# Differential-attention scores as K=64 products on two halves of the array, and the value products ordered by operand

## Chip, cores and metric

The kernel runs on one core of a Trainium2 chip. The metric is the device time of one execution in microseconds.

## What is computed

One inference step of a two-layer encoder for 1024 prompt frames and 32 sample frames, with `D_MODEL` = 1024. Layer 0 mixes tokens by causal pooling, layer 1 by differential attention; both layers also attend to 256 memory tokens, and both end in a squared-ReLU MLP. The change lies in layer 1's differential attention on the prompt:

```python
def diff_core(q, k, v, q_pos, k_pos, lam, slopes):
    """q (B,Tq,H,2,d), k (B,Tk,H,2,d), v (B,Tk,H,2d). Returns (A1 - lam*A2) V, (B,Tq,H,2d)."""
    s = jnp.einsum('bqhcd,bkhcd->cbhqk', q, k).astype(jnp.float32) * (DIFF_HEAD_DIM ** -0.5)
    dist = jnp.abs(q_pos[:, None] - k_pos[None, :]).astype(jnp.float32)
    bias = -slopes[:, None, None] * dist[None]
    vis = (k_pos[None, :] // CHUNK) <= (q_pos[:, None] // CHUNK)
    s = jnp.where(vis, s + bias, -jnp.inf)
    p = jax.nn.softmax(s, axis=-1)
    a = p[0] - lam * p[1]
    return jnp.einsum('bhqk,bkhe->bqhe', a.astype(v.dtype), v)
```

There are 4 heads. Each has two components c = 0, 1 of d = 64 dimensions, so a head's query or key has 128 dimensions, [component 0 | component 1]. A score is a sum over 64 dimensions only; the values have 128.

## The kernel before

**Precision.** TensorE works on a type (`F32R`) that keeps only part of a float32. Every operand is therefore split in a high part, a copy made by ScalarE (ACT), and a low part, the operand less the high one, made by VectorE (DVE) or GpSimd (POOL): `split`, L55. A product is then three matmuls: high x high, high x low, low x high (`mm3`, L48 to L53). The low x low product is left out where `mm3` is used.

**Stages.** `run` (L1586) calls layer 0's mixing (`mix0`), its output projection and MLP (`tail`), then layer 1's mixing (`mix1`, L938) and its `tail`. The change is in `mix1` alone.

**Inside `mix1`.** The work is written as generators, which yield the time that they estimate to have put on TensorE (PE). `drive` (L527) steps through the units, which are the attention (`diff_unit`, L915, then the memory attention), and after each step takes about 0.8 times that estimate from a filler, `fill1` (L959): dense projections of 352 token columns (`g_dense`, L143), in PSUM tiles named `dn`. So scores and values are interleaved with dense work, in one order per engine that is fixed when the program is built; a scheduler still moves instructions past each other in that order.

For each head, `diff_project` (L685) makes keys `kst`, values `vst` and queries. For the queries, one 1024-column tile is kept for 256 tokens: `Q` has the shape [128, 2, 2, 256], for component, part (high, low) and token. Component c is split where it falls, on partitions 64c to 64c+63 (L728), and then copied by a DMA on the SP queue to the other 64 partitions (L734), so that all 128 partitions hold the 64 dimensions twice. `diff_keys` (L739) puts, for each component, the high part of the keys on one half of the partitions and the low part on the other (`KS`, [128, 2, 1024]).

`diff_scores` (L782) goes through blocks i = 0 to 7 of 128 queries, two to a `pair`; block i sees Wi = max(256, 128(i + 1)) keys. For each component it multiplies the stacked parts, so two matmuls of 128 rows give four products, low x low among them:

```python
nc.tensor.matmul(o, lhsT=q[:, c, 0, qc], rhs=KS[:, c, k:k + n], start=True, stop=False)
nc.tensor.matmul(o, lhsT=q[:, c, 1, qc], rhs=KS[:, c, k:k + n], start=False, stop=True)
```

(L799, L800.) Up to 512 keys are one chunk; more are two chunks of Wi/2. Each component takes one PSUM tile `sc` of two banks; there are two such tiles. DVE then adds the distance table and takes the extremum in one instruction (L806), ACT takes the exponential (L808), and `combine` (L777) subtracts the second component's probabilities, scaled, from the first's. A yield stands after each component.

`diff_values` (L823) transposes two blocks' probabilities on PE (L841), splits them into `ah` and `al` (DVE makes `al`), and multiplies with the split values `V` through `mm3`, one key block of 128 after the other: V high x ah, V high x al, V low x ah, then the same for the next block. These matmuls have 256 columns.

**Gates.** With `until`, the filler stops until a named score block is done, since query tiles (`q`, four buffers) must come free. Head h's queries wait pair by pair for head h-1's scores (L718). The memory queries wait at L962.

**Other work in PE's halves.** The sample group's scores (`diff_sample`, L878 and L879) multiply 64 rows at a time, component 0 on the lower half of the array's rows and component 1 on the upper, with 32 columns of weights; L903 uses 32 rows. Everything else of the kernel uses all 128 rows.

Of the kernel before, what the change touches and what calls it, by code (L numbers as in the profile page):

```python
# [9 lines left out]
F32 = mybir.dt.float32  # L10
F32R = mybir.dt.float32r
AF = mybir.ActivationFunctionType
ALU = mybir.AluOpType
# [3 lines left out]
SEQ = 1024  # L17
NS = 32
NT = SEQ + NS
GW = 352  # L20
# [7 lines left out]
SC_DIFF = 64.0 ** -0.5  # L28
# [5 lines left out]
STEPS = 44  # L34
LAG = 22
KEYS_AT = 1
T2_AT, T_AT = 8, 20
ORDER = (2, 0, 1)
YOFF = 896
# [3 lines left out]
class Kern:  # L43
# [292 lines left out]
    def mem_project(self, l, h, p, out, qs, gate=()):  # L336
        nc = self.nc
        W = self.weight()
        for key in gate:
            yield from self.until(key)  # L340
        q = [self.qp.tile([128, 2, 512], F32R, tag="q", name="mq", bufs=self.nq) for a in range(2)]
        for g in range(NG):
            ps = self.dntile()[:, :GW]
            yield from self.g_dense(ps, W, g)
            qf = p.tile([128, GW], F32, tag="qf", name="qf", bufs=2)
            nc.vector.tensor_tensor(qf, ps, self.rs[g], ALU.mult)
            for a, lo, hi in ((0, 0, 512), (1, 512, SEQ)):
                lo, hi = max(lo, g * GW), min(hi, (g + 1) * GW)
                if lo < hi:
                    s = slice(lo - 512 * a, hi - 512 * a)  # L350
                    self.split(q[a][:, 0, s], q[a][:, 1, s], qf[:, lo - g * GW:hi - g * GW], nc.gpsimd)
            if g == NG - 1:
                nc.gpsimd.tensor_copy(qs[:, h, :], qf[:, GW - NS:])
        out[h] = q

    def mem_load_kv(self, l, h, p):
        nc, t = self.nc, self.t
# [327 lines left out]
    def diff_project(self, h, p, out, smp):  # L685
        nc, t = self.nc, self.t
        W = self.weight()
        if h:
            yield from self.until(("ks", h - 1))
        kst = self.pd.tile([128, NT], F32, tag="kst", name="kst", bufs=1)  # L690
        for g in ORDER if h == 0 else range(NG):
            ps = self.dntile()[:, :GW]
            yield from self.g_dense(ps, W, g)
            nc.vector.tensor_tensor(kst[:, g * GW:(g + 1) * GW], ps, self.rs[g], ALU.mult)
        nc.sync.dma_start(t["kT"][h], kst)
        self.kst = kst
        self.done.add(("k", h))

        W = self.weight()
        if h:  # L700
            yield from self.until(("v", h - 1))
        vst = self.pd.tile([128, NT], F32, tag="vst", name="vst", bufs=1)
        for g in range(NG):
            ps = self.dntile()[:, :GW]
            yield from self.g_dense(ps, W, g)
            nc.vector.tensor_tensor(vst[:, g * GW:(g + 1) * GW], ps, self.rs[g], ALU.mult)
        nc.sync.dma_start(t["vT"][h], vst)

        W = self.weight()
        Q = []  # L710
        for g in range(NG):
            ps = self.dntile()[:, :GW]
            yield from self.g_dense(ps, W, g)
            qf = p.tile([128, GW], F32, tag="qf", name="qf", bufs=2)
            nc.vector.tensor_tensor(qf, ps, self.rs[g], ALU.mult)
            lo, end = g * GW, min((g + 1) * GW, SEQ)
            if h:
                yield from self.until(("s", h - 1, (end - 1) // 256))  # L718
            while lo < end:
                n = lo // 256  # L720
                hi = min(end, 256 * (n + 1))
                s = slice(lo - 256 * n, hi - 256 * n)
                if len(Q) == n:
                    Q.append(self.qp.tile([128, 2, 2, 256], F32R, tag="q", name="Q", bufs=self.nq))
                q = Q[n]
                for c in range(2):
                    b = slice(64 * c, 64 * c + 64)
                    self.split(q[b, c, 0, s], q[b, c, 1, s], qf[b, lo - g * GW:hi - g * GW], nc.gpsimd)  # L728
                lo = hi
                if hi == 256 * (n + 1):  # L730
                    qd = q.bitcast(F32)
                    for c in range(2):
                        b, o = slice(64 * c, 64 * c + 64), slice(64 - 64 * c, 128 - 64 * c)
                        nc.sync.dma_start(qd[o, c], qd[b, c])  # L734
            if g == NG - 1:
                nc.gpsimd.tensor_copy(smp["q"][:, h, :], qf[:, GW - NS:])
        out[h] = {"vst": vst, "Q": Q}

    def diff_keys(self, h, smp):  # L739

        nc = self.nc
        while ("k", h) not in self.done:
            yield 0.0
        kst = self.kst
        KS = self.pd.tile([128, 2, SEQ], F32R, tag="ks", name="KS", bufs=2)
        KSf = KS.bitcast(F32)
        for a in range(4):
            s = slice(256 * a, 256 * a + 256)
            nc.scalar.copy(KS[0:64, 0, s], kst[0:64, s])
            nc.scalar.copy(KS[64:128, 1, s], kst[64:128, s])  # L750
            nc.vector.tensor_tensor(KS[64:128, 0, s], kst[0:64, s], KSf[0:64, 0, s], ALU.subtract)
            nc.vector.tensor_tensor(KS[0:64, 1, s], kst[64:128, s], KSf[64:128, 1, s], ALU.subtract)
            yield 0.0
        self.KS[h] = KS
        nc.gpsimd.tensor_copy(smp["k"][:, h, :], kst[:, SEQ:])
        self.done.add(("ks", h))
# [25 lines left out]
    def diff_scores(self, h, pair, p, d, A):  # L782
        nc = self.nc
        Wk = 256 * (pair + 1)
        q = d["Q"][pair]
        KS = self.KS[h]
        for i in (2 * pair, 2 * pair + 1):
            qc = slice((i % 2) * 128, (i % 2) * 128 + 128)
            Wi = max(256, 128 * (i + 1))
            st = self.pd.tile([128, 8], F32, tag="std", name="std", bufs=4)  # L790
            prs = []
            for c in range(2):
                tile = self.sctile()
                n = Wi if Wi <= 512 else Wi // 2
                off = 512 - n if Wi > 512 else 0
                sc = tile[:, off:off + Wi]
                for k in range(0, Wi, n):
                    o = sc[:, k:k + n]
                    nc.tensor.matmul(o, lhsT=q[:, c, 0, qc], rhs=KS[:, c, k:k + n], start=True, stop=False)  # L799
                    nc.tensor.matmul(o, lhsT=q[:, c, 1, qc], rhs=KS[:, c, k:k + n], start=False, stop=True)  # L800
                if c:
                    pr = p.tile([128, Wk], F32, tag="p1", name="pr", bufs=1)
                else:
                    pr = (p if pair % 2 else self.pd).tile([128, Wk], F32, tag=f"pA{2 + pair % 2}", name="pr", bufs=2)
                y = YOFF - 128 * i
                nc.vector.tensor_tensor_reduce(out=pr[:, :Wi], in0=sc, in1=self.dtab[:, y:y + Wi], scale=-SC_DIFF,  # L806
                                               scalar=3e38, op0=ALU.add, op1=ALU.min, accum_out=st[:, c:c + 1])
                self.last_exp = nc.scalar.activation(pr[:, :Wi], pr[:, :Wi], AF.Exp, bias=st[:, c:c + 1],  # L808
                                                     scale=-1.0, accum_out=st[:, 4 + c:5 + c])
                prs.append(pr)  # L810
                if c == 0:
                    yield 0.22 * (pair + 1)
            nc.vector.reciprocal(st[:, 6:8], st[:, 4:6])
            nc.vector.tensor_scalar(st[:, 7:8], st[:, 7:8], self.lam, None, ALU.mult)
            self.combine(p, 128, Wi, prs[0], prs[1], st[:, 6:7], st[:, 7:8])
            if Wi < Wk:
                nc.gpsimd.memset(prs[0][:, Wi:], 0.0)
            A.append(prs[0])
            if i % 2:
                self.done.add(("s", h, pair))  # L820
            yield 0.22 * (pair + 1)

    def diff_values(self, h, pair, p, d, A):  # L823
        nc = self.nc
        V = d["V"]
        nk = 2 * (pair + 1)
        po = None
        for kk in range(0, nk + 2, 2):
            if kk:
                if po is None:  # L830
                    po = self.mmtile()[:, :256]
                for a in range(2):
                    k = kk - 2 + a
                    self.mm3(po, V[:, 0, k, :], V[:, 1, k, :], ah[:, 256 * a:256 * a + 256],
                             al[:, 256 * a:256 * a + 256], k == 0, k == nk - 1)
            if kk < nk:
                pt = self.mmtile()
                for a in range(2):
# [120 lines left out]
    def fill1(self, p, dd, qq, smp, qs):  # L959
        for h in range(4):  # L960
            yield from self.diff_project(h, p, dd, smp)
        gates = [[("s", 3, 1)], [("s", 3, 3)], [("m", 1, 0, 1)], [("m", 1, 1, 1)]]  # L962
        for h in range(4):
            yield from self.mem_project(1, h, p, qq, qs, gates[h])
        self.new_x(1)
# [715 lines left out]
```

## Time and profile before

| what | value |
|---|---|
| median of 3 runs | 2105.55 us (2105.54 to 2108.3) |
| the profiled execution | 2107.0 us |
| its span, first to last instruction | 2105.2 us |
| granted TensorE clock, mean | 0.997 |
| PE busy | 99% of the span, 13068 matmuls |
| DVE, ACT, POOL busy | 80%, 53%, 27% |

How to read it: L12 is line 12 of the kernel. PE is TensorE's matmuls, PEld its weight loads, which can run while an earlier matmul streams. Matmuls are pipelined, and one row's duration runs on while the next has started, so a busy PE is no measure of density: the distance of two starts is. A form like `64*32` behind a matmul says how many rows and columns of the array its weights take; `128x512` is the size of its result. "x12" merges twelve equal instructions, with the time from the first's start to the last's end. Idle time is given with the engine, tile and line that ended it ("<- DVE aTl L57"). `sc`, `mm` and `dn` are the PSUM tiles of scores, of transposes and values, and of dense work.

### The profile page before, as it was taken

The page shows a single profiled execution, that of the slowest core. Times are in us where ns is not written, and L with a number is a line of the kernel's source. Part 1 is how long each engine was busy: PE and PEld are TensorE (multiplying, and loading weights), DVE is VectorE, ACT ScalarE, POOL GpSimd, SP SyncE. Part 2 cuts the span into 40 slices and gives each one's busy share as a digit, 9 for nine tenths or more (in the row PEclk, how much of TensorE's full clock was granted, in tenths as well). Part 3 has the DMA queues.
Part 4 walks back from the last instruction along what each step waited for, and adds up shares of the span by engine and source line. Part 5 has one row for each costly group of instructions (what it writes and reads, how often), then busy time and mean ns, then how long its engine had stood idle before and what let it go on. Part 6 is the DMA issues. An engine that isn't in the chain of part 4 may idle for free. (4 is left out here: it accounts for less than half of the span.)

```text
span 2105.2 us, 35352 instructions
## 1 busy us (share of the span) xinstructions
PE 2081.7 (99%) x13068; PEld 2045.3 (97%) x13068; DVE 1683.4 (80%) x3164; ACT 1125.7 (53%) x2437; POOL 568.0 (27%) x577
## 2 busy tenths in 40 slices
PE   9999999999999999999999999999999999999998
PEld 8998999999999999999999998999999999999997
DVE  8856598888888888868778877589888888888865
ACT  7546365444444444456777766355544444444454
POOL 1021113333333333220111212104334333333323
PEclk9999999999999999999999999999999999999999
DMA  5634411111111111124222213411111111111112
GB/s 192 198 113 139 149 55 56 51 49 53 49 53 45 57 41 60 41 71 159 77 79 79 83 37 99 160 51 51 56 46 54 48 51 51 48 53 50 52 41 83
DMA packets 88269, 156.85 MB, mean 75 GB/s; under 512 B 12832, under 2 KB 30880, under 8 KB 87584
## 3 DMA queue, kind: packets, MB, share of 16 engines
q1 hardware_dynamic: 86224, 149.61, 22.3%
q10 hardware_dynamic: 1872, 4.98, 0.8%
q8 instruction: 102, 1.67, 0.3%
q14 instruction: 71, 0.58, 0.1%
HBM read 126.64 MB, written 23.72 MB: 71 GB/s over the span
## 5 line engine op out<-in xcount | busy, mean ns | idle before, releaser
L51 PE MATMUL dn<-xh,whi 128*128 128x352 f32 x1168 | 383.8, 329 | 2.9 <-ACT xh L229 1.1
L52 PE MATMUL dn<-xl,whi 128*128 128x352 f32 x1168 | 379.0, 324 | 0.4 <-DVE xl L230 0.4
L53 PE MATMUL dn<-xh,wlo 128*128 128x352 f32 x1168 | 378.9, 324 | 0.0
L109 DVE TENSOR_TENSOR wlo<-wraw,whi 128x512 fp32r<-128x512 f32 x344 | 280.1, 817 | 83.6 <-ACT whi L108 82.8
L1375 DVE TENSOR_TENSOR x<-x,mm 128x352 f32<-128x352 f32 x560 | 287.5, 513 | 62.7 <-PE mm L53 62.6
L108 ACT CAST whi<-wraw 128x512 fp32r<-128x512 f32 x344 | 212.4, 620 | 232.4 <-PE dn L52 117.5
L51 PE MATMUL mm<-h2h,whi 128*128 128x352 f32 x832 | 270.4, 325 | 0.0
L53 PE MATMUL mm<-h2h,wlo 128*128 128x352 f32 x832 | 268.0, 322 | 0.0
L52 PE MATMUL mm<-h2l,whi 128*128 128x352 f32 x832 | 266.4, 320 | 0.0
L108 ACT CAST whi<-ws 128x512 fp32r<-128x512 f32 x232 | 143.9, 620 | 220.3 <-PE dn L52 123.4
L1375 DVE TENSOR_TENSOR x<-x,xb 128x352 f32<-128x352 f32 x448 | 222.8, 511 | 26.1 <-PE xb L53 23.4
L51 PEld LDWEIGHTS dn<-xh,whi 128*128 128x128 f32 x1168 | 219.8, 188 | 8.4 <-issue 2.0
L52 PEld LDWEIGHTS dn<-xl,whi 128*128 128x128 f32 x1168 | 221.0, 189 | 3.1 <-DVE xl L230 1.3
L53 PEld LDWEIGHTS dn<-xh,wlo 128*128 128x128 f32 x1168 | 220.4, 189 | 0.4
L57 POOL TENSOR_TENSOR h2l<-t,h2h 128x352 fp32r<-128x352 f32 x112 | 137.0, 1224 | 170.8 <-ACT h2h L56 170.8
L109 DVE TENSOR_TENSOR wlo<-ws,whi 128x512 fp32r<-128x512 f32 x232 | 179.0, 772 | 3.5 <-ACT whi L108 3.5
L57 POOL TENSOR_TENSOR h2l<-b,h2h 128x352 fp32r<-128x352 f32 x92 | 116.2, 1275 | 228.7 <-PE mm L53 204.0
L1359 POOL TENSOR_TENSOR t<-b,b 128x352 f32<-128x352 f32 x56 | 64.7, 1155 | 366.3 <-ACT b L1278 366.3
L52 PEld LDWEIGHTS mm<-h2l,whi 128*128 128x128 f32 x832 | 156.3, 188 | 0.4
L51 PEld LDWEIGHTS mm<-h2h,whi 128*128 128x128 f32 x832 | 156.1, 188 | 0.4
L53 PEld LDWEIGHTS mm<-h2h,wlo 128*128 128x128 f32 x832 | 156.2, 188 | 0.0
L53 PE MATMUL dn<-T,wlo 128*128 128x352 f32 x480 | 155.7, 324 | 0.0
(312 smaller groups left out, 5326.9 us busy)
## 6 DMA issues: line engine op xcount, KB each, us to landing
wraw<-in_w_ff SPq DMA_DIRECT2D x256, 256.0 KB, 2.6
wraw<-in_w_out SPq DMA_DIRECT2D x44, 256.0 KB, 3.6
wraw<-in_w_mem SPq DMA_DIRECT2D x32, 256.0 KB, 3.1
wraw<-in_w_in SPq DMA_DIRECT2D x30, 256.0 KB, 3.1
o<-oscr SPq DMA_DIRECT2D x36, 176.0 KB, 3.0
xscr<-x SPq DMA_DIRECT2D x3, 1408.0 KB, 4.7
wraw<-in_w_kv SPq DMA_DIRECT2D x16, 256.0 KB, 2.6
Q<-Q SPq DMA_DIRECT2D x32, 128.0 KB, 2.2
```

The source lines that it names most:

```text
L51: mm(ps, lhsT=ah, rhs=bh, start=first, stop=False, skip_group_check=more)
L52: mm(ps, lhsT=ah, rhs=bl, start=False, stop=False, skip_group_check=more)
L53: self.last_mm = mm(ps, lhsT=al, rhs=bh, start=False, stop=last, skip_group_check=more)
L57: (lo_eng or self.nc.vector).tensor_tensor(lo, src, hi.bitcast(F32), ALU.subtract)
L108: self.nc.scalar.copy(hi, src)
L109: eng.tensor_tensor(lo, src, hi.bitcast(F32), ALU.subtract)
L1359: self.nc.gpsimd.tensor_tensor(h[out], h[a], h[c], ALU.subtract)
L1375: nc.vector.tensor_tensor(xj, xj, ps, ALU.add)
```

## The change

Queries and keys are no longer stacked. `Q` is [128, 2, 512], high and low for 512 tokens, split over all 128 partitions at once (the helper `split_q`, cut out of `mem_project`); the copies between halves are gone. `KS` is split the same way, in two pieces of 512 keys. A score now takes three products of 64 rows for each component, high x high, high x low, low x high; the two components stand on rows 0 to 63 and 64 to 127, and are issued in turn, each into its own PSUM bank. Low x low is no longer part of it. Both components are issued before the first of them is read; up to 512 keys they share one `sc` tile, above that they take both. The yields change from 0.22 to 0.25 per pair index. The gates follow the two query tiles a head: head h's queries wait for head h-2's last pair, and the first memory queries for head 2's last pair. `diff_values` writes its products by operand: V high x ah for both key blocks, V low x ah for both, V high x al for both.

```diff
+Y0, Y1 = 0.25, 0.25
...
+    def split_q(self, q, qf, g):
+
+        for a, lo, hi in ((0, 0, 512), (1, 512, SEQ)):
+            lo, hi = max(lo, g * GW), min(hi, (g + 1) * GW)
+            if lo < hi:
+                s = slice(lo - 512 * a, hi - 512 * a)
+                self.split(q[a][:, 0, s], q[a][:, 1, s], qf[:, lo - g * GW:hi - g * GW], self.nc.gpsimd)
...
-        Q = []
+        if h > 1:
+            yield from self.until(("s", h - 2, 3))
+        Q = [self.qp.tile([128, 2, 512], F32R, tag="q", name="Q", bufs=self.nq) for a in range(2)]
...
-                for c in range(2):
-                    b = slice(64 * c, 64 * c + 64)
-                    self.split(q[b, c, 0, s], q[b, c, 1, s], qf[b, lo - g * GW:hi - g * GW], nc.gpsimd)
-                lo = hi
-                if hi == 256 * (n + 1):
-                    qd = q.bitcast(F32)
-                    for c in range(2):
-                        b, o = slice(64 * c, 64 * c + 64), slice(64 - 64 * c, 128 - 64 * c)
-                        nc.sync.dma_start(qd[o, c], qd[b, c])
+            self.split_q(Q, qf, g)
...
-        for a in range(4):
-            s = slice(256 * a, 256 * a + 256)
-            nc.scalar.copy(KS[0:64, 0, s], kst[0:64, s])
-            nc.scalar.copy(KS[64:128, 1, s], kst[64:128, s])
-            nc.vector.tensor_tensor(KS[64:128, 0, s], kst[0:64, s], KSf[0:64, 0, s], ALU.subtract)
-            nc.vector.tensor_tensor(KS[0:64, 1, s], kst[64:128, s], KSf[64:128, 1, s], ALU.subtract)
+        for a in range(0, SEQ, 512):
+            s = slice(a, a + 512)
+            self.split(KS[:, 0, s], KS[:, 1, s], kst[:, s])
...
+            if Wi > 512:
+                sc = [self.sctile()[:, 512 - n:512 - n + Wi] for c in range(2)]
+            else:
+                tile = self.sctile()
+                sc = [tile[:, 512 * c:512 * c + Wi] for c in range(2)]
+            for k in range(0, Wi, n):
+                for m, (u, v) in enumerate(((0, 0), (0, 1), (1, 0))):
+                    for c in range(2):
+                        b = slice(64 * c, 64 * c + 64)
+                        nc.tensor.matmul(sc[c][:, k:k + n], lhsT=q[b, u, qc], rhs=KS[b, v, k:k + n],
+                                         start=m == 0, stop=m == 2)
...
-                for k in range(0, Wi, n):
-                    o = sc[:, k:k + n]
-                    nc.tensor.matmul(o, lhsT=q[:, c, 0, qc], rhs=KS[:, c, k:k + n], start=True, stop=False)
-                    nc.tensor.matmul(o, lhsT=q[:, c, 1, qc], rhs=KS[:, c, k:k + n], start=False, stop=True)
...
-                    yield 0.22 * (pair + 1)
+                    yield Y0 * (pair + 1)
...
-                for a in range(2):
-                    k = kk - 2 + a
-                    self.mm3(po, V[:, 0, k, :], V[:, 1, k, :], ah[:, 256 * a:256 * a + 256],
-                             al[:, 256 * a:256 * a + 256], k == 0, k == nk - 1)
+                for u, part in ((0, ah), (1, ah), (0, al)):
+                    for a in range(2):
+                        k = kk - 2 + a
+                        nc.tensor.matmul(po, lhsT=V[:, u, k, :], rhs=part[:, 256 * a:256 * a + 256],
+                                         start=kk == 2 and a == u == 0 and part is ah,
+                                         stop=kk == nk and part is al and a == 1)
...
-        gates = [[("s", 3, 1)], [("s", 3, 3)], [("m", 1, 0, 1)], [("m", 1, 1, 1)]]
+        gates = [[("s", 2, 3)], [("s", 3, 3)], [("m", 1, 0, 1)], [("m", 1, 1, 1)]]
```

In the changed program the scores' line is L786, the value products' L824, the probabilities' transposes L832, the values' L752, and L52 to L54 are the former L51 to L53.

The next section places the change in the order of PE's instructions where its steps rest on it; the rows there are the program's own, and no time is in them.

More of the change, by code (lines that the diff above doesn't have):

```diff
@@ L346, in mem_project @@
             nc.vector.tensor_tensor(qf, ps, self.rs[g], ALU.mult)
[L347 to L351, printed above, removed]
+            self.split_q(q, qf, g)
             if g == NG - 1:
@@ L715, in diff_project @@
             nc.vector.tensor_tensor(qf, ps, self.rs[g], ALU.mult)
[L716 to L725, printed above, removed]
-                for c in range(2):
-                    b = slice(64 * c, 64 * c + 64)
-                    self.split(q[b, c, 0, s], q[b, c, 1, s], qf[b, lo - g * GW:hi - g * GW], nc.gpsimd)
-                lo = hi
-                if hi == 256 * (n + 1):
-                    qd = q.bitcast(F32)
-                    for c in range(2):
-                        b, o = slice(64 * c, 64 * c + 64), slice(64 - 64 * c, 128 - 64 * c)
-                        nc.sync.dma_start(qd[o, c], qd[b, c])
+            self.split_q(Q, qf, g)
             if g == NG - 1:
@@ L745, in diff_keys @@
         KS = self.pd.tile([128, 2, SEQ], F32R, tag="ks", name="KS", bufs=2)
-        KSf = KS.bitcast(F32)
-        for a in range(4):
-            s = slice(256 * a, 256 * a + 256)
-            nc.scalar.copy(KS[0:64, 0, s], kst[0:64, s])
-            nc.scalar.copy(KS[64:128, 1, s], kst[64:128, s])
-            nc.vector.tensor_tensor(KS[64:128, 0, s], kst[0:64, s], KSf[0:64, 0, s], ALU.subtract)
-            nc.vector.tensor_tensor(KS[0:64, 1, s], kst[64:128, s], KSf[64:128, 1, s], ALU.subtract)
+        for a in range(0, SEQ, 512):
+            s = slice(a, a + 512)
+            self.split(KS[:, 0, s], KS[:, 1, s], kst[:, s])
             yield 0.0
@@ L784, in diff_scores @@
         Wk = 256 * (pair + 1)
-        q = d["Q"][pair]
+        q = d["Q"][pair // 2]
         KS = self.KS[h]
         for i in (2 * pair, 2 * pair + 1):
-            qc = slice((i % 2) * 128, (i % 2) * 128 + 128)
+            qc = slice(128 * i - 512 * (pair // 2), 128 * i - 512 * (pair // 2) + 128)
             Wi = max(256, 128 * (i + 1))
             st = self.pd.tile([128, 8], F32, tag="std", name="std", bufs=4)
+            n = Wi if Wi <= 512 else Wi // 2
+            if Wi > 512:
[9 more added lines that the diff above has]
+                                         start=m == 0, stop=m == 2)
             prs = []
             for c in range(2):
[L793 to L796, printed above, removed]
-                for k in range(0, Wi, n):
-                    o = sc[:, k:k + n]
-                    nc.tensor.matmul(o, lhsT=q[:, c, 0, qc], rhs=KS[:, c, k:k + n], start=True, stop=False)
-                    nc.tensor.matmul(o, lhsT=q[:, c, 1, qc], rhs=KS[:, c, k:k + n], start=False, stop=True)
                 if c:
@@ L805, in diff_scores @@
                 y = YOFF - 128 * i
-                nc.vector.tensor_tensor_reduce(out=pr[:, :Wi], in0=sc, in1=self.dtab[:, y:y + Wi], scale=-SC_DIFF,
+                nc.vector.tensor_tensor_reduce(out=pr[:, :Wi], in0=sc[c], in1=self.dtab[:, y:y + Wi], scale=-SC_DIFF,
                                                scalar=3e38, op0=ALU.add, op1=ALU.min, accum_out=st[:, c:c + 1])
@@ L820, in diff_scores @@
                 self.done.add(("s", h, pair))
-            yield 0.22 * (pair + 1)
+            yield Y1 * (pair + 1)
     def diff_values(self, h, pair, p, d, A):
```

## The prediction, on record before the changed kernel ran

> **What bounds the kernel now.** I read the page's first part, then the busy time by stage, then the waits of TensorE in the stage that is edited, then single rows of that stage in order of time.
>
> ```profile
> PE 2081.7 (99%) x13068; PEld 2045.3 (97%) x13068; DVE 1683.4 (80%) x3164; ACT 1125.7 (53%) x2437; POOL 568.0 (27%) x577
> ```
>
> The stages (from:to, length, busy time and instructions of PE, PEld, DVE, ACT, POOL, clock, DMA); the differential attention runs from 985 to 1240 us:
>
> ```profile
> 985.00:1240.00 255.00, 252.32 (x1628) 241.32 (x1633) 201.88 (x523) 182.59 (x456) 40.22 (x77) 1.00 0.27 84
> 1240.00:1335.00 95.00, 92.55 (x609) 84.14 (x598) 64.48 (x136) 56.65 (x166) 18.88 (x29) 0.98 0.33 109
> ```
>
> And what PE waited for from 985 to 1240 us (total, times, longest):
>
> ```profile
> PE mm L52 <- DVE aTl L57: 0.7, 2, 0.4
> PE mm L772 <- DVE std L813: 0.6, 1, 0.6
> PE dn L51 <- DVE kst L694: 0.5, 1, 0.5
> PE sc L799 <- DVE std L806: 0.2, 1, 0.2
> ```
>
> PE is idle for 255.00 - 252.32 = 2.7 us of the stage, at a full clock. So whatever the edit takes off DVE, ACT, POOL or the queues can return 2.7 us at most; the rest is decided by PE's own time. The score products, and how densely PE streams, stand here: the two lines by shape, then nine rows in order of time (start, duration, instruction).
>
> ```profile
> L799 PE MATMUL sc<-KS,Q x96: 278/346/527, 1015.8 to 1228.1; 128*128 128x384 f32 x24, 128*128 128x512 f32 x24, 128*128 128x256 f32 x16, 128*128 128x320 f32 x16
> L800 PE MATMUL sc<-KS,Q x96: 277/340/532, 1015.9 to 1228.3; 128*128 128x384 f32 x24, 128*128 128x512 f32 x24, 128*128 128x256 f32 x16, 128*128 128x320 f32 x16
> ...
> 1225.10 0.39 PE L799 MATMUL sc<-KS,Q 128*128 128x512 f32 x1
> 1225.33 0.40 PE L800 MATMUL sc<-KS,Q 128*128 128x512 f32 x1
> 1225.57 0.39 PE L799 MATMUL sc<-KS,Q 128*128 128x512 f32 x1
> 1225.79 0.40 PE L800 MATMUL sc<-KS,Q 128*128 128x512 f32 x1
> 1226.03 0.32 PE L51 MATMUL dn<-xh,whi 128*128 128x352 f32 x1
> 1226.19 0.32 PE L52 MATMUL dn<-xl,whi 128*128 128x352 f32 x1
> ```
>
> Durations overlap, so the price of a matmul is the distance of two starts: (1226.03 - 1225.10)/4 = 0.2325 us for 512 columns, 0.16 for 352, both 0.454 ns a column, with the weight load hidden. The widths of one line, the remaining 16 matmuls being 448 wide by the loop, sum to 24x384 + 24x512 + 16x(256 + 320 + 448) = 37,888 columns; two lines make 75,776, or 34.4 us.
>
> **Part 1, the products.** Now six products of 64 rows replace four of 128 for each chunk. Do two halves run at once? The sample's scores at L878 already use both halves in turn: two rows over the first 0.06 us, the loads of the same spot, and what one such matmul takes alone.
>
> ```profile
> 1236.34 0.41 PE L878 MATMUL sc<-kvc,qsd 64*32 64x256 f32 x2
> ...
> 1236.33 0.15 PEld L878 LDWEIGHTS sc<-kvc,qsd 64*32 64x32 f32 x4 [0.18 <-DVE rs_r L215]
> ...
> L878 PE MATMUL sc<-kvc,qsd x16: 376/388/400, 1236.3 to 1240.1; 64*32 64x256 f32 x16
> ```
>
> Two take 0.41 us together where one takes up to 0.40, and four loads are done in 0.15: the halves compute and load side by side. Were all pairs kept, three slots would replace four: 25.8 us, a gain of 8.6. But the scheduler does not keep all. Head 3's block of 640 keys, with the tiles' numbers; before (L799, L800 are the scores, `sc_14253` and `sc_14270` components 0 and 1):
>
> ```order
> L799 MATMUL sc_14253<-KS_13625,Q_13931 128x320
> L800 MATMUL sc_14253<-KS_13625,Q_13931 128x320
> L799 MATMUL sc_14253<-KS_13625,Q_13931 128x320
> L800 MATMUL sc_14253<-KS_13625,Q_13931 128x320
> L52 MATMUL mm_14059<-aTl_14130,V_13501 128x256
> L53 MATMUL mm_14059<-aTh_14129,V_13501 128x256
> L51 MATMUL mm_14059<-aTh_14129,V_13501 128x256
> ```
>
> And now (L786 are the scores; `sc_14266` is component 0, `sc_14267` component 1):
>
> ```order
> L786 MATMUL sc_14228<-KS_13564,Q_13730 128x512
> L786 MATMUL sc_14266<-KS_13564,Q_13731 128x320 x6
> L52 MATMUL dn_14435<-xh0_11086,whi_13889 128x352
> ...
> L54 MATMUL dn_14435<-xh0_11086,wlo_13900 128x352
> L52 MATMUL dn_14435<-xh0_11086,whi_13899 128x352
> L53 MATMUL dn_14435<-xl0_11087,whi_13899 128x352
> L786 MATMUL sc_14267<-KS_13564,Q_13731 128x320 x6
> ```
>
> All six of component 0 stand alone, and component 1's come 18 dense matmuls and more later: unpaired, six slots. So it is for head 0's 640 keys (+640x3 columns = 0.87 us) and head 3's 640 to 1024 (+3328x3 = 4.54). In heads 1 and 2 pairs are cut in the middle, here at 384 and 512 keys of head 1. Before, a cut between products cost nothing:
>
> ```order
> L799 MATMUL sc<-KS,Q 128x384
> L841 MATMUL mm<-ident,pr 128x128 x4
> L800 MATMUL sc<-KS,Q 128x384
> L799 MATMUL sc<-KS,Q 128x384
> L800 MATMUL sc<-KS,Q 128x384
> ```
>
> Now:
>
> ```order
> L786 MATMUL sc<-KS,Q 128x384 x5
> L824 MATMUL mm<-aTh,V 128x256 x4
> L786 MATMUL sc<-KS,Q 128x384
> ...
> L786 MATMUL sc<-KS,Q 128x512
> L824 MATMUL mm<-aTh,V 128x256 x4
> L786 MATMUL sc<-KS,Q 128x512 x2
> L824 MATMUL mm<-aTl,V 128x256 x2
> ```
>
> Each cut at an odd place adds a slot: 384, 512 and 320 columns, 0.55 us a head, 1.1 for both. Sum: 25.8 + 0.87 + 4.54 + 1.1 = 32.3 us. **The products save 34.4 - 32.3 = 2.1 us**, not 8.6. Bounds: -2.1 if pairs are perfect, and 6 x 18,944 columns x 0.454 = 51.7, so +17.2, if none is.
>
> **Part 2, going in and out of the halves.** Through the whole PE order the 288 matmuls of L786 stand in 48 unbroken runs (9, 12, 12 and 15 by head), with full-array work on both sides. What one such visit costs is seen where two small half-array matmuls (L879) stand between full ones; PE first, then the loads:
>
> ```profile
> 1238.58 0.28 PE L52 MATMUL sc<-mk,mq 128*128 128x256 f32 x1
> 1238.70 0.28 PE L53 MATMUL sc<-mk,mq 128*128 128x256 f32 x1
> 1238.82 0.28 PE L51 MATMUL mm<-aTh,V 128*128 128x256 f32 x1
> 1239.03 0.24 PE L879 MATMUL sc<-ksd,qsd 64*32 64x32 f32 x2
> 1239.20 0.39 PE L51 MATMUL sc<-mk,mq 128*128 128x256 f32 x1
> 1239.42 0.28 PE L52 MATMUL sc<-mk,mq 128*128 128x256 f32 x1
> ...
> 1238.70 0.19 PEld L51 LDWEIGHTS mm<-aTh,V 128*128 128x128 f32 x1
> 1239.02 0.13 PEld L879 LDWEIGHTS sc<-ksd,qsd 64*32 64x32 f32 x2
> 1239.20 0.19 PEld L51 LDWEIGHTS sc<-mk,mq 128*128 128x128 f32 x1
> 1239.31 0.19 PEld L52 LDWEIGHTS sc<-mk,mq 128*128 128x128 f32 x1
> ```
>
> Full matmuls of 256 columns start every 0.12 us, and a load begins one matmul ahead (1238.70 for 1238.82). Going in, L51 has streamed by 1238.94, yet the load of L879 begins only at 1239.02: 0.08 of drain. Coming out, L51's load begins at 1239.20, with its matmul, and the next starts 0.22 later: 0.10 of load in the open. From 1238.82 to 1239.42 are 0.60 us; less two matmuls of 0.12 and the two small ones (32 columns each, some 0.03 apiece) leaves 0.30. Those two loaded 32 columns; a load of 128 leaves 0.10 open where 32 leave about 0.03, so a visit costs about 0.38. A second place has 128 columns on both sides, L903 on 32 rows between L902:
>
> ```profile
> 1273.85 0.29 PEld L903 LDWEIGHTS mm<-dsT,vsd 32*128 32x128 f32 x2
> 1274.18 0.52 PEld L902 LDWEIGHTS mm<-dsT,kvc 128*128 128x128 f32 x4
> 1274.74 0.29 PEld L903 LDWEIGHTS mm<-dsT,vsd 32*128 32x128 f32 x2
> ```
>
> Here loads are never hidden and follow at (0.52 - 0.19)/3 = 0.11; the round of six takes 1274.74 - 1273.85 = 0.89 where six loads make 0.66: 0.23 for both drains. With two loads of 0.10 newly in the open that is 0.43. I take 0.39, between the two places: **48 x 0.39 = +18.7 us**. Bounds: the drains alone, 0.18, give +8.6; nothing gives 0. The Trainium skill's page TensorEngine Tiling (Tiling Modes, Key Properties) states that a change of tiling mode drains the array, without a figure; by the drain alone the sum would take the 8.6, but the rows above show the reload in the open too, and they decide.
>
> **Part 3, the rest.** The values' products stay 240 of 256 columns; both that need `al` now come last, so the 0.7 us at L52 <- aTl goes, up to 1.2 counting matmuls that started late: -1.0. The keys' splits shrink on ACT and DVE (32 half-height DVE operations of 0.42 us to 8 of full height), Q's 48 splits on POOL to 16, and 32 copies of 128 KB leave SP's queue:
>
> ```profile
> L751 DVE TENSOR_TENSOR KS<-kst,KS x16: 418/419/421, 989.9 to 1147.8; 64x256 fp32r<-64x256 f32 x16
> L734 SPq DMA_DIRECT2D Q<-Q x32: 461/467/550, 1010.1 to 1189.2; - x32
> L806 DVE CUSTOM_DVE_ANT_0 pr<-sc,dtab x64: 410/748/1219, 1016.6 to 1233.0; 128x256 f32<-128x256 f32 x16, 128x384 f32<-128x384 f32 x8, 128x512 f32<-128x512 f32 x8, 128x640 f32<-128x640 f32 x8
> ```
>
> All of it lies beside PE, which waits 2.7 us in the stage; I take -1.0 of that, no more, since DVE's critical work is L806. Against it, a block over 512 keys now takes both score tiles at once, so PE can wait for two L806 of up to 1.22 us before the next block; behind that wait stands all of PE's dense work. The order shows at least six other matmuls between such blocks, so +1.0, with 0 and +5 as ends. Q's gate now asks for head h-2's last pair, which is long done: nothing.
>
> **Sum:** -2.1 + 18.7 - 1.0 - 1.0 + 1.0 = +15.6 us. The profiled execution took 2107.0 (span 2105.2), so it would take 2122.6; the median of the runs, 2105.55, lies 1.45 lower, so the time is 2121.
>
> **Rivals.** (a) Drains alone count, the loads being taken ahead: -2.1 + 8.6 - 1.0 = +5.5, 2111. For it: loads are hidden everywhere in full mode; against: 1239.20 and 1239.31. Chance 0.12. (b) The other side: entering two halves of 128 columns costs nothing, because the pauses above belong to column tiles (L878, L879) and quarter rows (L903). Then only -2.1 - 1.0 and up to 2.7 of waits remain: 2101. It decides if a visit is under 3.1/48 = 0.06 us. Against it stand three places with 0.2 and more. Chance 0.07. The Trainium skill's TensorEngine Tiling (Overview, Theoretical Speedup) gives up to 2x for 64 rows; by that alone scores would halve their product time and 2096 result, but the order above pairs only part. (c) Loads of the two halves follow each other: +0.10 a run and, below 470 columns, slots of 0.21: about +9.6, 2131. Against: four loads in 0.15. Chance 0.07. (d) The halves do not overlap at 128 columns: +17.2 instead of -2.1, 2140. Chance 0.04. My forecast has 0.70.
>
> **The numbers.** 0.2% is 4.2 us, about what a measurement of this kernel can tell. Faster comes from (b) alone: 0.05; same from the rest of (b) and the low end of (a): 0.06; slower 0.89. The range runs from the drains-only case with a little luck, 2109, to (c), 2131.
>
> **What would show it.** Right: L786 in 48 runs, pairs starting within 0.03 us of each other, spacing 0.23 for 512-wide pairs; before and after each run a start some 0.2 us late, PE's waits in the stage under 4 us, and the whole difference inside the attention stage. Wrong: runs entered with no pause (b), second starts 0.1 or a whole matmul late (c, d), or waits of L786 for L795 (the new L806) over 5 us.

## The result, and the profile after

| | before | changed |
|---|---|---|
| median of 4 runs each | 2105.86 us (2105.54 to 2108.3) | 2123.31 us (2121.3 to 2124.68) |
| ratio | | 1.0080, 95% interval 1.0062 to 1.0097 |
| profiled execution, its span | 2107.0, 2105.2 us | 2121.3, 2119.4 us |

The change costs 17.5 us by the medians and 14.3 by the two profiled executions. Forecast were 2121 and a range of 2109 to 2131. Here is the changed kernel's first part of the page:

```profile
PE 2096.9 (99%) x13164; PEld 2044.8 (96%) x13164; DVE 1677.1 (79%) x3140; ACT 1109.2 (52%) x2381; POOL 550.9 (26%) x545
```

PE has 96 matmuls more and 15.2 us more of busy time; every other engine has less. Cut at nearly the same events, the beginning of layer 1's mixing and 774 us ahead of the end, the stages of the changed kernel are (from:to, length, busy time of PE, PEld, DVE, ACT, POOL, clock, DMA):

```profile
0.00:985.00 985.00, 979.64 (x6151) 966.27 (x6152) 794.58 (x1437) 510.02 (x1081) 261.01 (x254) 1.00 0.26 84
985.00:1345.00 360.00, 354.65 (x2305) 319.47 (x2303) 256.61 (x625) 221.36 (x563) 41.36 (x73) 1.00 0.22 72
1345.00:2119.00 774.00, 762.64 (x4712) 759.11 (x4711) 625.88 (x1080) 377.78 (x738) 248.54 (x219) 0.99 0.18 57
```

and of the kernel before:

```profile
985.00:1331.00 346.00, 341.01 (x2207) 321.90 (x2207) 263.40 (x652) 236.89 (x617) 57.31 (x104) 1.00 0.28 87
1331.00:2105.00 774.00, 763.26 (x4724) 759.90 (x4722) 627.62 (x1083) 379.00 (x740) 249.50 (x219) 0.99 0.18 57
```

The whole difference, 360 - 346 = 14 us, lies in layer 1's mixing. PE's idle time there is the same, 360.00 - 354.65 = 5.4 us and 346.00 - 341.01 = 5.0. So the time went into PE's own stream. One visit to the halves in the changed kernel shows where, in order of time: six products of the block of 512 keys in head 0, first PE, then PE cut to the run's beginning, then the loads.

```profile
1020.85 0.32 PE L53 MATMUL dn<-xl,whi 128*128 128x352 f32 x1
1021.00 0.32 PE L54 MATMUL dn<-xh,wlo 128*128 128x352 f32 x1
1021.26 0.98 PE L786 MATMUL sc<-KS,Q 64*128 64x512 f32 x6
1022.17 0.43 PE L52 MATMUL dn<-xh,whi 128*128 128x352 f32 x1
1022.43 0.32 PE L53 MATMUL dn<-xl,whi 128*128 128x352 f32 x1
...
1021.26 0.50 PE L786 MATMUL sc<-KS,Q 64*128 64x512 f32 x2
...
1020.85 0.19 PEld L54 LDWEIGHTS dn<-xh,wlo 128*128 128x128 f32 x1
1021.26 0.53 PEld L786 LDWEIGHTS sc<-KS,Q 64*128 64x128 f32 x6 [0.22 <-DVE std L803]
```

L54 of 352 columns has streamed 0.16 us after its start, at 1021.16; the next start is at 1021.26, with its load, so 0.09 to 0.10 of drain and no load ahead. The two halves start together and end within 0.50 us, so pairs do run side by side. The second pair has to wait for its load, too, so the three pairs have streamed by 1021.26 + 3 x 0.2325 + 0.11 = 1022.07; the full array starts at 1022.17, 0.10 later, which is the drain on the way out. Its first matmul keeps its successor waiting 0.26 instead of 0.16, the other open load. From 1021.16 to the successor at 1022.43, less L52's own 0.16, are 1.11 us; three pairs of 512 columns take 3 x 0.2325 = 0.70. **The visit costs 0.41.**

The same subtraction over all runs gives an account of the mixing. For each unbroken run of score products I take the time from the end of the full-array matmul ahead of it (its start plus 0.4545 ns a column, at least the 0.107 us of a load) to the start of the second full-array matmul behind it, less the first one's columns. What all other PE starts lie apart beyond their columns is "late starts elsewhere".

| kernel | runs | products by their columns | scores, measured | late starts elsewhere |
|---|---|---|---|---|
| before | | 34.4 | 38.3 | 15.5 |
| changed | 48 | 32.3 | 51.9 | 15.2 |

Scores rise by 13.6 us; late starts stay. If the products cost what their columns say, the 48 visits cost (51.9 - 32.3)/48 = 0.41 us each; the experiments test that split.

### The profile page after: what moved, and what is told of

Same layout as the page of the kernel before. It is cut to its first block, busy times and chain, and to the rows that moved or that the text cites. A ratio compares the mean times of both kernels' runs of the same rounds, so it can differ in the third digit from the quotient of the medians.

```text
span 2119.4 us, 35318 instructions
## 1 busy us (share of the span) xinstructions
PE 2096.9 (99%) x13164; PEld 2044.8 (96%) x13164; DVE 1677.1 (79%) x3140; ACT 1109.2 (52%) x2381; POOL 550.9 (26%) x545
## 4 chain that ended last, share of the span: by engine, by line
PE 88%; DVE 2%; ACT 2%; DMA 1%; issue 1%; POOL 0%; SPq 0%; DVEq 0%; ACTq 0%; POOLq 0%
PE dn L52 15%; PE dn L54 15%; PE dn L53 15%; PE mm L52 9%; PE mm L53 8%; PE mm L54 8%; PE xb L52 3%; PE xb L54 3%; PE xb L53 3%; PE sc L786 2%; PE mm L824 1%; PE mm L832 1%; PE sc L52 1%; PE sc L53 1%; PE sc L54 1%
## 5 line engine op out<-in xcount | busy, mean ns | idle before, releaser
L52 PE MATMUL dn<-xh,whi 128*128 128x352 f32 x1168 | 386.0, 331 | 1.8 <-DVE edge L605 0.9
L54 PE MATMUL dn<-xh,wlo 128*128 128x352 f32 x1168 | 379.5, 325 | 0.1
L53 PE MATMUL dn<-xl,whi 128*128 128x352 f32 x1168 | 379.3, 325 | 0.0
L52 PE MATMUL mm<-h2h,whi 128*128 128x352 f32 x832 | 270.4, 325 | 0.0
L54 PE MATMUL mm<-h2h,wlo 128*128 128x352 f32 x832 | 268.0, 322 | 0.0
L53 PE MATMUL mm<-h2l,whi 128*128 128x352 f32 x832 | 266.4, 320 | 0.0
L1366 DVE TENSOR_TENSOR x<-x,xb 128x352 f32<-128x352 f32 x448 | 223.2, 512 | 26.1 <-PE xb L54 23.4
L52 PEld LDWEIGHTS dn<-xh,whi 128*128 128x128 f32 x1168 | 220.1, 188 | 11.1 <-issue 5.9
L53 PEld LDWEIGHTS dn<-xl,whi 128*128 128x128 f32 x1168 | 221.2, 189 | 2.3 <-DVE xl L231 0.6
L54 PEld LDWEIGHTS dn<-xh,wlo 128*128 128x128 f32 x1168 | 220.3, 189 | 0.9 <-DVE wlo L110 0.4
L53 PEld LDWEIGHTS mm<-h2l,whi 128*128 128x128 f32 x832 | 156.3, 188 | 0.4
L52 PEld LDWEIGHTS mm<-h2h,whi 128*128 128x128 f32 x832 | 156.1, 188 | 0.4
L54 PEld LDWEIGHTS mm<-h2h,wlo 128*128 128x128 f32 x832 | 156.2, 188 | 0.0
L54 PE MATMUL dn<-T,wlo 128*128 128x352 f32 x480 | 155.7, 324 | 0.0
```

Source lines behind the costliest of these rows:

```text
L52: mm(ps, lhsT=ah, rhs=bh, start=first, stop=False, skip_group_check=more)
L53: mm(ps, lhsT=ah, rhs=bl, start=False, stop=False, skip_group_check=more)
L54: self.last_mm = mm(ps, lhsT=al, rhs=bh, start=False, stop=last, skip_group_check=more)
L1366: nc.vector.tensor_tensor(xj, xj, ps, ALU.add)
```

## The experiments

**Theory V**: visits to the half-array mode cost the time. **Rival U**: the products left without a partner do, and a visit costs little. **Rival W**: PE waits for both score tiles, or for DVE.

**One visit a block** (`e1_one_visit_a_block`). The first product of a block over 512 keys waits until DVE has read the score tiles of the block before (`last_red` is DVE's last such instruction), and the rest of every block goes ahead of other work:

```diff
-                    for c in range(2):
-                        b = slice(64 * c, 64 * c + 64)
-                        nc.tensor.matmul(sc[c][:, k:k + n], lhsT=q[b, u, qc], rhs=KS[b, v, k:k + n],
-                                         start=m == 0, stop=m == 2)
+                    for c in range(2):
+                        b = slice(64 * c, 64 * c + 64)
+                        first = k == m == c == 0
+                        with ExitStack() if first else self.tc.high_priority():
+                            mm = nc.tensor.matmul(sc[c][:, k:k + n], lhsT=q[b, u, qc], rhs=KS[b, v, k:k + n],
+                                                  start=m == 0, stop=m == 2)
+                        if first and i > 3:
+                            self.tc.add_manual_dep(mm.ins, self.last_red.name, mybir.DependencyInfo(
+                                mybir.DependencyClass.Sync, mybir.DependencyReason.DATA), reason="pairs")
...
+                self.last_red = red.ins
```

> The changed kernel, with each block's score products kept together: 32 unbroken runs instead of 48, every pair intact, so the products take 25.8 us of slots instead of 32.3. Theory V (each visit to the half-array mode costs 0.41 us, 0.09 of drain and 0.11 of open weight load on either side): before + (25.8 - 34.4) + 32 x 0.41 = before + 4.5, about 2110. Rival U (only the unpaired products cost, visits nothing measurable): 6.5 us off the changed kernel, about 2117. Rival W (the time went into waits of PE for both score tiles): every block over 512 keys now waits for both tiles before its first product, so no gain, 2123 or more.

Measured 2116.96 us, ratio to before 1.0059 (1.0043 to 1.0076): the total of rival U. The account tells another story: the scores take 39.3 us, where V forecasts 25.8 + 32 x 0.41 = 38.9 and U 51.9 - 6.5 = 45.4. But late starts elsewhere rise from 15.2 to 23.4, and 8 of the 12.6 us are given back. What PE waits for most in the mixing of this run, from 985 to 1341 us (total, times, longest; L830 are the value products, `mk` the keys of the memory attention, which follows the differential one):

```profile
PE sc L52 <- ACT mk L57: 4.0, 2, 3.4
PE mm L830 <- DVE aTl L58: 2.8, 8, 1.1
PE mm L830 <- ACT aTh L57: 1.4, 4, 0.5
PE mm L830 <- DVE rs_r L216: 0.6, 1, 0.6
```

In the changed kernel the wait for `mk` is 0.4 us and that for `aTl` 3.4. So V holds for the scores. W does not hold for the total: it had 2123 or more, no matmul of the scores is among PE's waits in this stretch, and the waits for `aTl` did not grow. What grew most is the wait for ACT's `mk`, 3.6 of the 8.2 us, most of it a single wait of 3.4 behind the differential attention; why ACT is later there is not shown. U fits the total only by accident.

**Two blocks a visit** (`e7_two_blocks_a_visit`). As above, and blocks 0 and 1, and 2 and 3, are multiplied in one go. Two more things differ from the run above: the products are kept in the program's order among themselves, and the first products of the small blocks wait for DVE as well.

```diff
+            if i not in got:
+                products(i, True)
+                if pair < 2:
+                    products(i + 1, False)
+            sc, Wi = got[i]
...
```

> As the run with one visit a block, but for the first four blocks of a head the products of two blocks share one visit: 24 runs, 25.8 us of slots. Theory V: 8 visits fewer, 3.3 us under the run with one visit a block, before + 1.2, about 2107. Rival U: no difference to the run with one visit a block, 2117. Rival W: later than it, since two blocks of scores are held at once.

Measured 2111.67 us, 1.0034 (1.0021 to 1.0048). With eight visits fewer the scores take 3.4 us less, 39.3 to 35.9 (V: 3.3; U: 0). The total falls by 5.3; that is not the visits alone, since the wait for `mk` is 0.5 here instead of 4.0 while others grew. V's total, about 2107, is missed again: the scores are now below the 38.3 of before, but late starts elsewhere, 22.9, are 7.4 above the 15.5 of before, and the kernel is still slower.

**A tiny half-array product** (`e3_tiny_half_array`) **and its control** (`e4_tiny_full_array`), both added to the kernel before. The scores' first product overwrites the result, so the outputs are untouched.

```diff
                 sc = tile[:, off:off + Wi]
+                nc.tensor.matmul(sc[:, :32], lhsT=q[0:64, c, 0, qc], rhs=KS[0:64, c, 0:32], start=True, stop=True)
```

The control has `q[:, c, 0, qc]` and `KS[:, c, 0:32]`.

> The kernel before, with one added product of 64 rows, 128 columns of weights and 32 columns of data ahead of each component's scores, 64 in all; the scores overwrite its result. Theory V: 64 visits of 0.41, and 0.02 for the product itself: +27 us, 2133. Rival U: a product in half mode costs no more than the same product in full mode, so as the run with full rows, 2112 or so. Rival W says nothing of it: +0 to +7.

> Control for the run with half rows: the same 64 added products of 32 columns, but on all 128 rows, so that the array's mode never changes. All theories: one load of 0.11 us cannot hide behind 32 columns, so 64 x 0.11 = +7 us, 2113.

Measured 2127.8 us (ratio 1.0110, 1.0094 to 1.0125) and 2114.33 (1.0045, 1.0030 to 1.0060). The half rows cost 13.5 us more than the same product on full rows, where V forecast 20 and U nothing. So a change of mode costs by itself, and U does not hold. One place in the run with half rows, then one in the control:

```profile
1040.38 0.32 PE L53 MATMUL dn<-xh,wlo 128*128 128x352 f32 x1
1040.62 0.28 PE L797 MATMUL sc<-KS,Q 64*128 64x32 f32 x1
1040.83 0.47 PE L800 MATMUL sc<-KS,Q 128*128 128x448 f32 x1
1041.14 0.36 PE L801 MATMUL sc<-KS,Q 128*128 128x448 f32 x1
```

```profile
1042.96 0.18 PE L797 MATMUL sc<-KS,Q 128*128 128x32 f32 x1
1042.99 0.45 PE L800 MATMUL sc<-KS,Q 128*128 128x448 f32 x1
1043.28 0.36 PE L801 MATMUL sc<-KS,Q 128*128 128x448 f32 x1
```

With half rows, 1040.38 to 1041.14 are 0.76 us, of which L53 and L800 need 0.16 + 0.20: 0.40 for one visit. In the control 1042.96 to 1043.28 are 0.32, less 0.20: 0.12, one open load. Over all 64 the account gives (61.7 - 38.3)/64 = 0.37 and (45.4 - 38.3)/64 = 0.11; the difference is 0.26 where V had 0.30. Taken place by place from the starts, the median of the 64 is 0.41 with half rows and 0.11 in the control, so the single visit has the forecast price; the sums differ by less, since some places of the control also wait for other things, up to 0.43 us. Late starts elsewhere fell as well, from 15.5 to 12.5 and 14.1, which accounts for part of what V's total is off by.

**Component by component** (`e2_component_by_component`): in the changed kernel `for c` moves outside `for k` and `for m`.

> The changed kernel with all products of component 0 ahead of those of component 1: still 48 runs, but hardly a pair side by side; slots of 47.2 us instead of 32.3. If the halves overlap as the prediction has it: +14.9 us on the changed kernel, about 2138. If they did not overlap in the changed kernel either: no difference, 2123.

Measured 2126.38 us, 1.0097 (1.0083 to 1.0110), some 3 us on the changed kernel, with intervals that overlap: neither forecast. The scores rise by 6.9 us, to 58.8, not by 14.9, so a run is not worked off in the order written. Head 0's 1024 keys, six of component 0 and then six of component 1 in the program, take these spans; this run, then the changed kernel:

```profile
1047.02 2.24 PE L786 MATMUL sc<-KS,Q 64*128 64x512 f32 x12
```

```profile
1046.81 1.66 PE L786 MATMUL sc<-KS,Q 64*128 64x512 f32 x12
```

Twelve one after the other would start over 11 x 0.2325 = 2.56 us. Even if the second half's first product started together with the first half's last, the starts would lie over 10 x 0.2325 = 2.33 us, and the last would end later still. So the second half's products begin while some of the first half's still stand ahead of them. Pairing matters, 0.58 us here; late starts elsewhere fall to 10.6, which hides part of it in the total.

**The values' order alone** (`e5_values_by_operand_alone`: the change's loop over `u, part` put into the kernel before; `e6_halves_values_by_block`: the changed kernel with `mm3` as before).

> The kernel before with the values' products by operand and nothing else. The prediction's term: -1.0 us (between -0.5 and -1.5), since both products that need the low part come last: 2105. Rival: holding the two low-part products together moves the wait for DVE behind four products instead of one and costs PE order elsewhere; in the changed kernel PE waits 3.4 us in three places for the low part: +1 to +3, 2107 to 2109.

> The changed kernel with the values' products block by block, as before; 48 runs of scores, slots of 32.2 us. By the prediction's term for the values +1.0 us, about 2124; by the rival, that the order by operand makes the 3.4 us of waits, -1 to -3, about 2121.

Measured 2105.45 us, ratio 1.0003 (0.9994 to 1.0012), and 2121.6, 1.0077 (1.0064 to 1.0089, against 1.0062 to 1.0097 with the new order). The order by itself does nothing that can be measured, either way. PE's longest waits in the changed kernel's attention are for `al`:

```profile
PE mm L824 <- DVE aTl L58: 3.4, 3, 1.1
PE dn L52 <- DVE kst L699: 0.5, 1, 0.5
```

They come from DVE's queue; here DVE ahead of one of them, and PE at its end:

```profile
1041.29 1.01 DVE L765 SCALAR_TENSOR_TENSOR pr<-pr,std 128x768 f32<-128x768 f32 x1
1042.21 1.08 DVE L795 CUSTOM_DVE_ANT_0 pr<-sc,dtab 128x896 f32<-128x896 f32 x1
1043.22 0.08 DVE L795 DVE_READ_ACCUMULATOR2_ANT std<- 128x1 f32 x1
1043.22 0.69 DVE L58 TENSOR_TENSOR aTl<-mm,aTh 128x512 fp32r<-128x512 f32 x1
...
1042.19 0.64 PE L824 MATMUL mm<-aTh,V 128*128 128x256 f32 x4
1043.96 0.50 PE L824 MATMUL mm<-aTl,V 128*128 128x256 f32 x2 [1.14 <-DVE aTl L58]
```

Two passes of DVE, over 768 probabilities and 896 scores a row, stand ahead of the 0.69 us that PE waits for; four products between `aTh` and `aTl` cover 0.47 us of that. With the values' order of before in the same kernel (`e6_halves_values_by_block`) PE waits there as long, 4.0 against 3.4 us in a single profile of each:

```profile
PE mm L53 <- DVE aTl L58: 4.0, 5, 1.2
```

**More or less dense work between blocks** (`f1_two_blocks_more_filler`, `f2_two_blocks_less_filler`: the run with two blocks a visit, `Y0, Y1` at 0.35 and at 0.15), **and its values block by block** (`f3_two_blocks_values_by_block`, with `mm3` as before).

> The run with two blocks a visit (24 visits, products of 25.8 us), with yields of 0.35 instead of 0.25, so more dense work between the score blocks. In that run the scores took 35.9 us of PE, 2.4 less than before, but PE waited 7.7 us more elsewhere. If those waits come from too little dense work between a block's scores and its values, more of it takes 3 to 7 us off, 2105 to 2109; if they come from the order that the kept-together products force, no change, 2112.

> The same with yields of 0.15. By the first reading 3 us or more slower than with 0.25, 2115; by the second no change, 2112.

> The run with two blocks a visit, with the values' products block by block as before. If the waits for the values' low part are a matter of their order, 1 to 3 us faster, 2109 to 2111; by what the two runs on the values' order alone showed, no change within 1 us.

Measured 2112.27 (1.0031, 1.0020 to 1.0042), 2112.12 (1.0026, 1.0014 to 1.0037) and 2117.91 us (1.0054, 1.0039 to 1.0069). The amount of dense work does not matter, which excludes the first reading. The second forecast just that, but which part of the forced order costs is not shown. In the third, against my expectation, the order by operand is worth some 4 us by the ratios (1.0054 against 1.0034) and some 6 by the medians once the scores are kept together. PE's waits there:

```profile
PE mm L53 <- DVE aTl L58: 4.2, 8, 1.1
PE sc L52 <- ACT mk L57: 2.2, 1, 2.2
PE sc L789 <- DVE std L812: 1.0, 3, 0.4
```

In a single profile of each, PE waits 1.4 us more at `aTl` (2.8 in the run with two blocks), 1.7 more at `mk` (0.5 there) and 0.8 more at the scores (0.2 there); since other waits shrink, its idle time in the mixing grows by 2.7 us only (6.9 to 9.6), about half of what is to be explained. For the rest I have no cause. No variant beats the kernel before.

## Why the prediction was right, step by step

- **Which engine decides.** Right. DVE, ACT, POOL and DMA all got less work, and PE's idle time did not move (5.0 and 5.4 us). But the 2.7 us of idle time were no bound on what other engines can cost PE or give back: a late start can hide under a row that runs on, and the account has 15.5 us of late starts outside the scores. In this change they moved by 0.3 only; in the runs with whole pairs they moved by 7 to 8.
- **Products, -2.1 us.** The halves do run side by side, and the cuts in the order cost about what they were counted at: with whole pairs, where no cut is left, the price of a visit comes out the same (next item).
- **Visits, 48 x 0.39 = +18.7.** Measured 0.41, 19.6 us in all; the same 0.41 to 0.42 in the kernels with 32 and 24 runs ((39.3 - 25.8)/32, (35.9 - 25.8)/24). The Trainium skill's page TensorEngine Tiling (Tiling Modes, Key Properties) names the drain alone. The trace agrees on the drain, some 0.09 each way; the two open loads are the other half, as the prediction had it.
- **The scores before, taken as 34.4.** Mis-sized: 38.3 with what stood around them. The full-array products had late starts of their own, 3.9 us, which the sum left out; in the changed kernel what stands around the scores is all in the 0.41 a visit. The scores' difference is thus +13.6 and not +16.6.
- **The rest, -1.0.** Late starts elsewhere moved by -0.3. The -1.0 for the values' order has no measurable counterpart (1.0003), and the waits for `aTl` that were to go, 0.7 us, are 3.4 in the changed kernel. The +1.0 for both score tiles did not appear as such either: no wait of the scores is among the long ones. A likely reason, which no run isolates, is that the scheduler issued one component alone where it held the other tile not to be free; the need for two tiles would then show as pairs left apart.
- **Sum.** The account gives 13.6 - 0.3 = 13.3, and the profiled executions differ by 14.3; the medians differ by 17.5. The profiled run of the changed kernel is the fastest of its four (2121.3 to 2124.68), and no trace shows where the other 3 us went. The forecast of +15.6 is 2.3 above the account: the scores came 3.0 lower and the rest 0.7 higher than forecast. That it lies within 2 us of the medians is in part luck.
- **Rivals.** (b), entry for nothing, is excluded by the added tiny products, 13.5 us apart. (a), drains alone, would be 0.18 a visit; measured 0.41. (c): both halves' loads begin together at 1021.26, (d): two products end in 0.50 us; both are excluded.

## What to carry to other kernels

Count visits before products: here one trip into half-array mode and back costs 0.41 us, as much as 900 columns of full-array streaming, so a block must save that many columns. A block of whole pairs saves as many as it has keys: by columns alone 896 keys break even, and only 1024 gain. The full-array products give up late starts of their own as well, 3.9/32 = 0.12 us a block here, so the estimate for this kernel falls to some 640 keys; with two small blocks to a visit the scores did get cheaper, 35.9 against 38.3. Look in the instruction order how often the mode would change and whether partners stay adjacent; a loop that issues them in turn does not settle it. Forcing them together took 16.0 us off the scores (51.9 to 35.9) and brought 7.7 of late starts elsewhere; that the work in between had been covering waits for DVE and ACT fits the waits listed above, but is not shown for all of it.

## What the runs showed that I had not expected

TensorE took the second half's products ahead of waiting ones of the first: with six and six in the program, the twelve started over 1.84 us (the last one's own 0.39 makes the 2.24) where strict order needs 2.33 at least. PE from 1047.0 us on, cut at 1047.59 and at 1047.62:

```profile
1047.02 0.73 PE L786 MATMUL sc<-KS,Q 64*128 64x512 f32 x2
1047.02 1.07 PE L786 MATMUL sc<-KS,Q 64*128 64x512 f32 x4
```

The third and the fourth start within 0.03 us, although starts of one half lie 0.23 or more apart; so the fourth belongs to the other half, ahead of three products that stand before it in the program. The trace does not name the halves; this is inferred from the starts.

And where the order is not forced, PE's time for scores and its late starts elsewhere trade: 38.3 and 15.5 us before, 45.4 and 14.1 with the tiny full-array products, 61.7 and 12.5 with the tiny half-array ones; 51.9 and 15.2 in the changed kernel, 58.8 and 10.6 component by component. So part of a longer PE stream came off its late starts, and the total grew by less. The two kernels with whole pairs do not lie on such a line by their scores alone (39.3 and 23.4, 35.9 and 22.9): there the late starts came with the forced order.
